# A tuned matmul with batch normalisation on one core: one more small transfer at the head, 64 words of x read through ScalarE's queue

## The chip, the core and the metric

The kernel runs on one core of a Trainium2 chip. The metric is device time in microseconds (us) of one execution, as a median of several executions of the same kernel. The kernel before was measured three times: 205.70, 205.74 and 206.15 us, median 205.74 us. The profile is of one execution, recorded on the chip.

## What is computed

```python
y = np.matmul(x, weight)                             # x: 16 x 512 x 1024, weight: 1024 x 768, float32
mean = np.mean(y, axis=(0, 1), keepdims=True)
var = np.var(y, axis=(0, 1), keepdims=True)
return gamma * (y - mean) / np.sqrt(var + eps) + beta
```

x is 8192 rows of 1024 words (33.5 MB), the weights are 3.1 MB, the result is 8192 x 768 words (25.2 MB). The statistics of each of the 768 columns run over all 8192 rows, so no row of the result can be written before the whole product is known.

## The kernel before

**Tiles.** The 8192 rows are worked on as 16 chunks of 512 rows (`CH`, `C`). The 768 columns are six tiles of 128. For the first two column tiles the product is made with rows on the partitions (`mm_rows`, line L510: x is the loaded operand, the weights are the moving one); for the other four with columns on the partitions (`mm`, L575: the weights are loaded, x is moving). The inner dimension of 1024 is cut into four quarters of 256 (`KQ`), each on 32 partitions, and each quarter into four steps (`jw`) of two halves (`e`): eight matmuls of 128 deep add up to one result.

**Loads.** GpSimd (POOL) issues all loads of x and of the weights, and each of them turns float32 into bf16 on its way. `load_x` (L403) makes four transfers of a group of rows, one for each quarter of the inner dimension, and puts them into `ring`; `load_quarter` (L387) moves one quarter of the weights for two of the four `jw` into `w_sb`. The order at the head, written out in the list `order`, with two weight quarters put in by `BETWEEN`, is: weights quarter 0 and 1 (first half of `jw`), x rows 0 to 255 in four transfers, weights quarter 2 and 3, x rows 256 to 511, the second half of the weights, x rows 512 to 767, rows 768 to 1023, and then whole chunks of 512 rows. A transfer of 256 rows reads 1 KB of each row and writes 512 bytes; its packets are counted as "128 KB". A weight transfer is counted as "192 KB", in packets of 3072 bytes. POOL's transfers share eight completion semaphores in turn, so that the ninth waits until the first has landed, and so on.

**Turning x.** VectorE (DVE) turns 32x32 blocks of the loaded x, so that the inner dimension stands on the partitions (`turn_x`, L435 and L428). The first 512 rows are turned in halves of `jw`.

**The order of work.** A planner in the kernel (`arrange`) takes tasks with costs and due times and writes one instruction order for each engine. `seq` fixes that order. The few instructions ahead of the planner's tasks (memsets, the activation below, the four small reads of the weights) stand in the program by hand, and the planner doesn't know of them.

**The head by hand.** ScalarE (ACT) has one small activation (`warm`, L346) whose table load comes with it; nothing reads `warm`. SyncE (SP) then issues four small reads of the weights into a tile `touched` (L350): for each quarter the first word of the rows in the first half of `jw`, 64 words in each transfer. Nothing reads `touched`. TensorE (PE) runs 16 row pieces of matmuls on a tile of zeros (`wake`, L591 and L594: 8 calls in float32, which show as 16, and 8 small ones in bf16) while the first data comes; two more such pieces stand between its first and second part of real work (`FILL`). Then comes `part(0, 1, ...)`: the first 256 rows with the first half of `jw`, first with L510, then with L575.

**Statistics and output.** ACT, DVE and POOL take squares, sums and bn_stats out of PSUM while PE goes on; ACT copies y to bf16 in SBUF. When a column tile's statistics are whole, its y is scaled and shifted, turned back (on PE against an identity, or by DMA transposes that SP issues), and SP stores it. The identity is made by POOL (`make_identity`) between its first loads, and ACT copies it to float32 (`ident32`, L457).

Of the kernel before, what the change touches and what calls it, by code (L numbers as in the profile page):

```python
# [227 lines left out]
def kernel(  # L228
# [9 lines left out]
    nc = tc.nc  # L238
    f32 = mybir.dt.float32
# [8 lines left out]
    P = 128  # L248
# [33 lines left out]
    x_flat = x.flatten_outer_dims()  # L282
    out_flat = out.flatten_outer_dims()

    singles = ctx.enter_context(tc.tile_pool(name="singles", bufs=1))
# [7 lines left out]
    def seq(bi):  # L293

        ins = bi.ins
        prev = last.get(ins.engine)
        if prev is not None:
            tc.add_manual_dep(
                ins, prev,
                mybir.DependencyInfo(mybir.DependencyClass.NoSync, mybir.DependencyReason.DATA),  # L300
                reason="order",
            )
        last[ins.engine] = ins.name
        return bi
# [38 lines left out]
    base = singles.tile([P, 2], f32)  # L343
    fss = singles.tile([P, 2], f32)

    seq(nc.scalar.activation(warm, eps_sb, AF.Sqrt))  # L346
    touched = singles.tile([P, 2, TOUCH], f32)
    first_rows = weight.rearrange("(i jw c e) n -> i c jw (e n)", i=4, jw=JW, e=2)
# [990 lines left out]
    for c, r0, rows in ends:  # L1339
        due = E + 2.0 + 0.6 * c  # L1340
        n = max(rows // CH, 1)
# [70 lines left out]
```

## Time and profile before

| | |
|---|---|
| device time, median of 3 | 205.74 us (205.70 to 206.15) |
| span of the profiled execution, first to last instruction | 204.07 us |
| time around the span (median less span; the profiled execution has no time of its own on record) | 1.67 us |
| PE busy | 189.3 us, 93% of the span |
| DVE, ACT, POOL busy | 78%, 72%, 61% |
| loads: POOL's queue | 18.36 MB as written, in 34624 packets |
| mean granted TensorE clock | 0.979 |

All times inside the profile count from the first instruction of the span. A slice of the page's rows is a fortieth of the span, 5.1 us. "DMA" in such rows is the busy share of the 16 DMA engines, and GB/s counts the bytes that were written: for loads of x and of the weights half the bytes that were read, since they become bf16. L-numbers are lines of the kernel before; in the changed kernel the lines behind the insertion are higher by three.

### The profile page before, as it was taken

The page shows a single profiled execution, that of the slowest core. Times are in us where ns is not written, and L with a number is a line of the kernel's source. Part 1 is how long each engine was busy: PE and PEld are TensorE (multiplying, and loading weights), DVE is VectorE, ACT ScalarE, POOL GpSimd, SP SyncE. Part 2 cuts the span into 40 slices and gives each one's busy share as a digit, 9 for nine tenths or more (in the row PEclk, how much of TensorE's full clock was granted, in tenths as well). Part 3 has the DMA queues.
Part 4 walks back from the last instruction along what each step waited for, and adds up shares of the span by engine and source line. Part 5 has one row for each costly group of instructions (what it writes and reads, how often), then busy time and mean ns, then how long its engine had stood idle before and what let it go on. Part 6 is the DMA issues. An engine that isn't in the chain of part 4 may idle for free.

```text
span 204.1 us, 3510 instructions
## 1 busy us (share of the span) xinstructions
PE 189.3 (93%) x1210; PEld 114.5 (56%) x1210; DVE 159.3 (78%) x250; ACT 146.2 (72%) x260; POOL 124.1 (61%) x150
## 2 busy tenths in 40 slices
PE   7969999999999999999999999999999999997900
PEld 3457554657488888777865444444444445544600
DVE  4031879999999999969989998987999878657900
ACT  2001461368989999899978766999998959956950
POOL 7776954877499989997403999389613312940000
PEclk9999999999999999999999999999999999999965
DMA  4999999999999999999686899899999999999998
GB/s 71 172 199 196 176 196 196 196 197 197 190 193 197 197 196 196 196 197 195 103 181 200 297 339 336 248 301 328 295 322 227 336 303 274 347 343 310 310 347 253
DMA packets 98562, 48.74 MB, mean 239 GB/s; under 512 B 24304, under 2 KB 98032, under 8 KB 98544
## 3 DMA queue, kind: packets, MB, share of 16 engines
q0 software_dynamic: 34624, 18.36, 65.5%
q1 hardware_dynamic: 63920, 30.16, 52.6%
q8 instruction: 9, 0.15, 0.3%
q14 instruction: 9, 0.07, 0.1%
HBM read 36.71 MB, written 25.17 MB: 303 GB/s over the span
## 4 chain that ended last, share of the span: by engine, by line
PE 86%; ACT 3%; DMA 3%; POOL 2%; issue 1%; ACTq 0%; DVE 0%; POOLq 0%
PE y_ps L575 54%; PE y_ps L510 24%; PE y_ps L814 4%; ACT o_sb L1361 3%; DMA ring<-in_x_dram 3%; PE o_ps L1044 1%; POOL ring L403 1%; POOL w_sb L387 1%; PE y_ps L753 1%; PE a_ps L903 1%; PE o_ps L1074 0%; ACTq L1407 0%; PE idle_ps L591 0%; PE tot_ps L871 0%; ACT ring L1252 0%
## 5 line engine op out<-in xcount | busy, mean ns | idle before, releaser
L575 PEld LDWEIGHTS <-w_sb 128*128 128x128 bf16 x520 | 50.3, 97 | 57.6
L575 PE MATMUL y_ps<-xT_sb,w_sb 128*128 128x512 bf16 (+1 forms) x272 | 59.3, 371 | 0.0
L575 PE MATMUL y_ps<-x_pl,w_sb 128*128 128x512 bf16 x248 | 57.4, 379 | 0.0
L403 POOL DMA_DIRECT2D ring<-in_x_dram x76 | 47.2, 626 | 14.4 <-DMA ring<-in_x_dram 5.5
L510 PE MATMUL y_ps<-w_sb,xT_sb 128*128 128x256 bf16 x448 | 50.6, 273 | 1.7 <-DMA ring<-in_x_dram 1.6
L510 PEld LDWEIGHTS <-xT_sb 128*128 128x128 bf16 x448 | 43.5, 98 | 9.4 <-DVE xT_sb L435 2.9
L435 DVE STREAM_TRANSPOSE xT_sb<-ring 128x1024 f32<-128x1024 f32 (+1 forms) x29 | 31.2, 1111 | 14.1 <-DMA ring<-in_x_dram 13.9
L711 DVE BATCH_NORM_STATS2 stats<-y_ps 128x6 f32<-128x512 f32 x46 | 30.9, 687 | 7.7 <-PE y_ps L575 7.2
L715 ACT CAST y_sb<-y_ps 128x512 bf16<-128x512 f32 x51 | 29.0, 593 | 10.4 <-DVE stats L711 6.3
L547 ACT COPY x_pl<-xT_sb 128x1024 bf16<-128x1024 bf16 x32 | 32.8, 1063 | 1.7 <-DVE xT_sb L435 1.7
L942 POOL TENSOR_TENSOR ring<-ring,sum 128x1024 f32<-128x1024 f32 (+1 forms) x11 | 23.8, 2188 | 14.9 <-ACT y_ps L724 10.9
L659 ACT ACTIVATE sq_sb<-y_ps 128x512 f32<-128x512 f32 x28 | 16.3, 610 | 16.2 <-PE y_ps L510 15.9
L666 POOL TENSOR_TENSOR sum<-sum,sq_sb 128x512 f32<-128x512 f32 x20 | 25.6, 1278 | 3.0 <-ACT sq_sb L659 1.7
L662 DVE TENSOR_TENSOR sum<-y_ps,sum 128x512 f32<-128x512 f32 x28 | 18.9, 675 | 6.3 <-ACT sq_sb L659 5.3
L672 ACT CAST y_sb<-y_ps 128x512 bf16<-128x512 f32 x28 | 16.3, 594 | 8.2 <-DVE sum L662 8.0
L1178 POOL TENSOR_TENSOR ring<-ring,sum 128x1024 f32<-128x1024 f32 x6 | 14.8, 2477 | 9.8 <-issue 8.5
L937 DVE TENSOR_TENSOR ring<-y_sb,a_ps 128x1024 f32<-128x1024 bf16 (+1 forms) x16 | 16.7, 1079 | 0.1
L1044 PE MATMUL o_ps<-ident,y_sb 128*128 128x128 bf16 x104 | 13.1, 221 | 1.6 <-DVE y_sb L1348 1.5
L1232 ACT CAST ring<-ring 128x1024 f32<-128x1024 bf16 x13 | 13.8, 1063 | 0.6 <-DMA ring<-y_sb 0.6
L1145 POOL COPY sum<-sum 32x256 f32<-32x256 f32 (+1 forms) x17 | 5.8, 340 | 13.4 <-DVE sum L1142 6.5
L428 DVE STREAM_TRANSPOSE xT_sb<-ring 128x2048 bf16<-128x2048 bf16 x6 | 13.5, 2290 | 0.1
L591 PE MATMUL idle_ps<-idle_sb 128*128 128x512 f32 x18 | 9.6, 688 | 1.5 <-DVE idle_sb L316 1.5
(104 smaller groups left out, 153.7 us busy)
## 6 DMA issues: line engine op xcount, KB each, us to landing
out_dram<-ring SPq DMA_DIRECT2D x37, 512.0 KB, 3.4
ring<-in_x_dram POOLq DMA_DIRECT2D x52, 256.0 KB, 8.8
out_dram<-o_sb SPq DMA_DIRECT2D x6, 512.0 KB, 4.7
ring<-in_x_dram POOLq DMA_DIRECT2D x16, 128.0 KB, 5.9
w_sb<-in_weight_dram POOLq DMA_DIRECT2D x8, 192.0 KB, 6.2
out_dram<-ring SPq DMA_DIRECT2D x6, 256.0 KB, 3.0
ring<-in_x_dram POOLq DMA_DIRECT2D x4, 192.0 KB, 7.8
out_dram<-o_sb SPq DMA_DIRECT2D x3, 256.0 KB, 2.5
```

Source lines behind the costliest of these rows:

```text
L403: bi = seq(nc.gpsimd.dma_start(x_bf[32 * i:32 * i + 32], src[:, :, KQ * i:KQ * (i + 1)]))
L435: seq(nc.vector.transpose(dst, src[:, :, jw0:jw1]))
L510: seq(nc.tensor.matmul(y_ps[:, s], x_of(c, jw, e, t * P, (t + 1) * P), w_sb[:, jw, e, 0:NA], start=(s == 0 and jw == 0 and e == 0), stop=( ...
L547: seq(nc.scalar.copy(dst, pairs) if eng == "ACT" else ENG[eng].tensor_copy(dst, pairs))
L575: seq(nc.tensor.matmul(y_ps, w_sb[:, jw, e, nt * P:(nt + 1) * P], moving(c, jw, e, q0 * QR, q1 * QR, parted), start=(jw == 0 and e == 0 an ...
L659: seq(nc.scalar.activation(sq_sb[:, 0:n], slot.tile[:, 0:n], AF.Square))
L662: seq(nc.vector.tensor_add(sum1, slot.tile[:, 0:n], sum1))
L666: seq(ENG[eng].tensor_add(acc, acc, state["sq"][:, 0:n]))
L711: seq(nc.vector.bn_stats(dst, slot.tile))
L715: seq(nc.scalar.copy(y(nt, c), slot.tile))
L937: seq(nc.vector.tensor_mul(slot.o, y_row[c].y[:, s0:s1], aff[0][:, None, :].to_broadcast([P, n, NA])))
L942: seq(ENG[eng].tensor_add(slot.o, slot.o, row[:, None, :].to_broadcast([P, n, NA])))
```

## The change

Three lines are put ahead of ScalarE's `warm` activation. They make a tile of 128 words, take the first word of every sixteenth row of x's first 1024 rows (64 words, 64 KB apart in memory), and let ScalarE's queue read them into 64 partitions of the tile. Nothing reads the tile.

```diff
     fss = singles.tile([P, 2], f32)
 
+    woken = singles.tile([P, 1], f32)
+    words = x_flat[0:1024, 0:1].rearrange("(h e s) n -> e h (s n)", h=4, e=16)
+    seq(nc.scalar.dma_start(woken[0:64], words[:, :, 0:1]))
     seq(nc.scalar.activation(warm, eps_sb, AF.Sqrt))
```

In the built program the order of instructions on PE, DVE, POOL and SP is the same as before. ACT has one instruction more, ahead of its table load. The completion semaphores of SP's and ACT's transfers are dealt out in turn from one set of eight, so each of SP's transfers now uses the next one of the set, and waits for the transfer that stands as many places back as before, with the new one counted in.

## Prediction

> **What bounds the kernel now.** I first read the page: busy shares, rate of the transfers, and the chain that ended last.
>
> ```profile
> span 204.1 us, 3510 instructions
> ...
> PE 189.3 (93%) x1210; PEld 114.5 (56%) x1210; DVE 159.3 (78%) x250; ACT 146.2 (72%) x260; POOL 124.1 (61%) x150
> ...
> GB/s 71 172 199 196 176 196 196 196 197 197 190 193 197 197 196 196 196 197 195 103 181 200 297 339 336 248 301 328 295 322 227 336 303 274 347 343 310 310 347 253
> ...
> PE 86%; ACT 3%; DMA 3%; POOL 2%; issue 1%; ACTq 0%; DVE 0%; POOLq 0%
> ```
>
> PE is the chain; transfers hold only 3% of it. In the loading phase they run at 196, except in the first two slices and the fifth. Next, PE's waits in the whole trace, and the chain's pieces at the head (start, length, what):
>
> ```profile
> PE y_ps L510 <- DMA ring<-in_x_dram: 1.6, 1, 1.6
> PE o_ps L1044 <- DVE y_sb L1348: 1.5, 1, 1.5
> PE idle_ps L591 <- DVE idle_sb L316: 1.5, 1, 1.5
> ```
> ```profile
> 5.32 0.53 POOL w_sb L387
> ...
> 5.98 6.13 DMA ring<-in_x_dram
> 12.11 0.03 issue
> 12.14 1.03 PE y_ps L510 x8
> ```
>
> After 12.14 PE never again waits for a load. So what the head takes, the kernel takes, us for us, and a head that ends earlier moves everything behind it. The chain names x as the releaser, but the first weight load and matmul of L510 need all four weight quarters, and the fourth was issued at 5.32. The weight transfers' landing, in the stretch that holds the third and fourth:
>
> ```profile
> L387 POOL DMA_DIRECT2D w_sb<-in_weight_dram x2: 534/536/538, 4.8 to 5.3; - x2
> ...
> DMA to landing us min/median/max: 6.3/6.5/6.7
> ```
>
> The fourth quarter landed at 5.32 + 6.7 = 12.0, just ahead of PE's first weight load at 12.11. x's first rows had landed by 10.14 (the fourth transfer, issued at 4.2, took 5.9) and were turned from 10.26 to 11.56. So the head is a queue of transfers in one order: two weight quarters, four of x, two weight quarters. The fourth quarter lands when the bytes before it are through. How fast were they (window; DVE's busy time; clock; share; GB/s)?
>
> ```profile
> 3.60:5.00 1.40, 0.00 (x0) 1.00 1.14 202
> 5.00:6.00 1.00, 0.00 (x0) 1.00 1.15 152
> 6.00:7.00 1.00, 0.00 (x0) 1.00 0.82 91
> 7.00:8.00 1.00, 0.00 (x0) 1.00 1.37 180
> 8.00:9.00 1.00, 0.00 (x0) 1.00 1.37 206
> ...
> 22.00:23.00 1.00, 1.00 (x2) 1.00 1.05 144
> ```
>
> There is a hole at 5 to 8, and the queue was not empty: eight transfers had been issued by 5.85. The trace's packet records place it: x's first packet is written at 5.19, and in the hole single packets of x take 738 and 693 ns, where they later take 60. In the whole load of x I find only one more such hole, at 22 to 25 (144, 171, 179 GB/s in the three windows of 1 us), where the 4096th packet, the end of row 1023, goes by. There a 16 KB instruction fetch at 22.3 takes a part; other such fetches cost about 10 KB of the stream, this hole some 88.
>
> **The change, part by part.**
>
> *ACT's issue.* One DMA instruction ahead of the table load (0.73 to 2.01). Nearest rows: SP's four issues took 403 to 427 ns each, POOL's up to 682 ns. An issue from ACT is not in this trace; I take 0.42. `warm` then ends near 2.65 instead of 2.23. ACT's next work is `ident32` at 7.00, after 4.77 us of idling for POOL's identity. Cost 0; the cover is gone only if the issue takes over 4.7 us.
>
> *The new packets.* SP's four touches made 320 four-byte packets, 80 each (64 words and 16 completions), so the new one makes 80, five for each DMA engine. They took 8 ns each while nothing else ran (1.75 to 2.54) and 22 ns between weight packets. The first weight packet is written at 2.69. The first touch, issued at 0.74, landed after 1.6, at 2.3; a read that ACT issues at 0.73 can be through by then: cost 0. If it is late: 5 x 22 ns = 0.11 us.
>
> *SP's touches.* If SP and ACT hinder each other in issuing, each touch comes up to 0.42 later. The second's packets (1.96 to 2.54) then fall among the first weights': another 0.11. The third and fourth already do (landing after 3.5 and 4.1 us). Upper bound of both 0.2; I take 0.
>
> [...]
>
> *Semaphores, later work.* The instruction order is the same on PE, DVE, POOL and SP. SP's completion semaphores move on by one; its next transfers, gamma's, land from 53.5 us on, long after all of these. Cost 0.
>
> *What it may remove.* The words lie 64 KB apart over exactly the rows between the two holes. If the first hole is a cost of reading a stretch of x for the first time, the touch pays it at 1.7 to 2.7, while the DMA engines wait for the first weights anyway. Size against 194 GB/s (the rate at 21 to 22 and 16 to 17 is 192 to 202): 5 to 6 lacks 42 KB, 6 to 7 lacks 103, 7 to 8 lacks 14; 159/194 = 0.82 us. In 5 to 6 the last touches, the weights' end and x's start mix, so I count on 6 to 8: 117/194 = **0.60 us**. Bounds: 0 and 0.82.
>
> *What is late next.* The fourth quarter at 11.4 instead of 12.0 still lands after x is turned (11.56 less 0.6 is 10.96). PE's filler ends at 10.56, so up to 1.5 could be gained. PE's second part starts at 15.85 behind its own two filler pieces (14.99), and DVE's next turn (14.85) hangs on the same queue, which moves as a whole. Nothing takes the gain back. The second hole stays, and PE does not wait there.
>
> *Sum.* 0 + 0 + 0 - 0.60 on a span of 204.07: 203.47. With the 1.67 that lie around the span, the median of 205.74 becomes **205.1 us**, if that part is the same; no row can look into it.
>
> **The rivals.**
>
> *A, the forecast: the hole is a first-read cost and goes.* For it: only two holes in 33.5 MB, one at the first row, one behind the last row that is touched; the same queue, packets and engines run at 192 to 197 elsewhere. 204.8 to 205.35. Chance 0.45.
>
> *B, the hole is not x's first read, or the touch doesn't remove it.* Against A: x's first transfer already visits all 256 rows, and 206 of its 256 packets were written by 6.0; the deepest second falls on the next transfer, 1 KB further in the same rows. The second half of the weights is not touched, and its first reading (13 to 17) shows no hole. And the first quarters, touched less than 1 us earlier, still began with packets of 735 to 992 ns instead of 247. POOL changes from issuing to computing at both holes too (identity at 5.84, L666 at 22.14), though its later L666 shows none. Then the change costs 0 to 0.2: 205.5 to 206.05, middle 205.75. Chance 0.38. [...]
>
> *C, slower: the touched words hold up the first weights.* The mechanism is a slow first read that stays in front of the weights in the DMA engines. Each engine would have four words of x, 1 MB apart. If a word takes the 0.6 us by which the first weight packets were long (835 in the middle, less 247) and they come one after the other, they last from 1.75 to 4.15. The weights, which else flow at full rate from about 3.5, lose 0.65 or more; if x's hole goes too, the two cancel, if it stays, the time is 206.4, and 206.6 with the 0.2 from above. It decides from a landing of the new transfer behind about 3.5 us. Against it: SP's first touch, on weights not read before, put out its 80 packets within 0.25 us. Chance 0.17, including what the unseen 1.67 us may add for a queue that was not in use.
>
> **How the numbers follow.** The likeliest is A: 205.1. Its own range is 204.8 to 205.35. The range for 8 in 10 takes in A and B, 204.8 to 206.1, and leaves C out. This kernel's measurement tells about 0.2%, 0.41 us, from no change. A lies beyond that nearly whole (0.03 of it within), a little of B could too: faster 0.43, same 0.40, slower 0.17.
>
> **What would show it.** Right: windows 6 to 7 and 7 to 8 near 194, no x packet over 400 ns there, the fourth quarter landing near 11.4, PE's first L510 near 11.5, all later pieces of the chain earlier by the same amount; the hole at 22 still there, 0.6 earlier. B: the 91 still stands at 6 to 7 and L510 starts at 12.1. C: the new transfer lands behind 3.5 us, and the first weight quarter later than the 5.0 of before. The forecast is wrong, too, if PE starts earlier and a wait for x or a slower span later takes the time back.

## The result and the profile after

The changed kernel takes **209.01 us** (median of 5 runs, 208.63 to 209.70) beside 205.82 (5 runs, 205.70 to 206.15): a ratio of 1.0146, interval 1.0126 to 1.0167, 3.2 us slower. The profiled execution took 209.70 with a span of 207.92, so 1.78 lie around the span; nothing is hidden there. Its page:

```profile
span 207.9 us, 3511 instructions
...
PE 189.4 (91%) x1210; PEld 114.6 (55%) x1210; DVE 159.5 (77%) x250; ACT 145.9 (70%) x260; POOL 124.2 (60%) x150
...
GB/s 76 156 198 196 182 196 196 187 194 196 190 194 196 197 198 194 196 197 193 92 154 198 383 340 266 261 339 312 313 290 214 309 318 328 345 345 285 281 285 184
...
PE 78%; DMA 9%; ACT 3%; POOL 2%; DVE 1%; issue 1%; ACTq 0%; DVEq 0%; POOLq 0%
```

PE, DVE, ACT and POOL have the same work and the same busy times as before, so what is new is waiting. The row of rates shows it in two places: the second slice has 156 instead of 172, and near the end, where before had 310 and 347, three slices have 281 to 285.

PE's waits and the pieces of its chain at the head (start, length, what):

```profile
PE y_ps L513 <- DMA ring<-in_x_dram: 1.9, 1, 1.9
...
PE y_ps L513 <- DVE xT_sb L438: 0.5, 1, 0.5
```
```profile
5.31 7.00 DMA w_sb<-in_weight_dram
```

The fourth weight quarter lands at 12.31 instead of 12.0, and PE's first L513 starts at 12.45, 0.31 later than before. At 26 us PE waits another 0.5 for a turned x. With these PE and ACT end their work 0.86 later. The remaining 3.0 of the 3.85 that the span grew lie behind the last matmul: from its start to the end of the span it is 13.2 us, where before had 10.2. There ACT still copies the last tiles of the result until 197.5 (before 196.7), and behind that only stores run. SP's issues (start, length, number), before and then after:

```profile
189.31 10.56 SPq L1364 DMA_DIRECT2D out_dram<-o_sb  x11
```
```profile
190.16 12.50 SPq L1367 DMA_DIRECT2D out_dram<-o_sb  x11
```

Two windows in which these eleven stores are the only transfers (window; DVE's busy time; clock; DMA share; GB/s), before and then after:

```profile
194.00:198.00 4.00, 0.00 (x0) 0.71 1.15 347
198.00:202.00 4.00, 0.00 (x0) 0.50 1.15 347
```
```profile
194.00:198.00 4.00, 0.50 (x2) 1.00 0.93 282
198.00:202.00 4.00, 0.00 (x0) 0.62 0.97 285
```

The stores start 0.85 later and then take 1.9 longer to issue: SP's queue waits for earlier stores of `o_sb` to land, 3.8 us at the longest where before had 1.5. They are the same stores of the same tile, `o_sb`, with 512-byte rows, at 0.81 of the rate (282/347). No instruction was added or moved there. What did move is an address. In the built program `fss`, with 8 bytes of each partition, starts at 66496, the new tile of one word at 66528, and `touched` behind it at 66560 instead of 66528: the new tile takes 32 bytes. It lies ahead of `touched`, and the pools opened behind the single tiles, with `o_sb`, `xT_sb`, `x_pl`, `y_sb` and `r_sb`, move as a whole: `o_sb`'s rows started at a multiple of 512 (66560) and now start at 66592, 32 bytes beyond one. `ring` and `w_sb` lie ahead of the tile and stay.

### The profile page after: what moved, and what is told of

Its sections match the earlier page's. It is cut to its first block, busy times and chain, and to the rows that moved or that the text cites. A ratio compares the mean times of both kernels' runs of the same rounds, so it can differ in the third digit from the quotient of the medians.

```text
span 207.9 us, 3511 instructions
## 1 busy us (share of the span) xinstructions
PE 189.4 (91%) x1210; PEld 114.6 (55%) x1210; DVE 159.5 (77%) x250; ACT 145.9 (70%) x260; POOL 124.2 (60%) x150
## 4 chain that ended last, share of the span: by engine, by line
PE 78%; DMA 9%; ACT 3%; POOL 2%; DVE 1%; issue 1%; ACTq 0%; DVEq 0%; POOLq 0%
PE y_ps L578 50%; PE y_ps L513 21%; DMA w_sb<-in_weight_dram 6%; PE y_ps L817 3%; DMA ring<-in_x_dram 3%; ACT o_sb L1364 3%; PE o_ps L1047 1%; POOL ring L406 1%; PE y_ps L756 1%; POOL w_sb L390 1%; DVE xT_sb L438 1%; PE a_ps L906 1%; PE o_ps L1077 0%; ACTq L1410 0%; PE tot_ps L874 0%
## 5 line engine op out<-in xcount | busy, mean ns | idle before, releaser
L513 PE MATMUL y_ps<-w_sb,xT_sb 128*128 128x256 bf16 x448 | 50.5, 273 | 2.5 <-DMA ring<-in_x_dram 1.9
L513 PEld LDWEIGHTS <-xT_sb 128*128 128x128 bf16 x448 | 43.6, 98 | 10.1 <-DVE xT_sb L438 3.5
```

The costliest lines, as they stand in the source:

```text
L513: seq(nc.tensor.matmul(y_ps[:, s], x_of(c, jw, e, t * P, (t + 1) * P), w_sb[:, jw, e, 0:NA], start=(s == 0 and jw == 0 and e == 0), stop=( ...
```

## The experiments

All ratios are to the kernel before, measured beside each kernel on the same chip. "Tail rate" is the rate in the two windows above, in GB/s; the rates in KB per us, in the expectations and below, count the same bytes in units of 1024, so that 347 GB/s are 339 KB per us.

| kernel | pools moved by | transfer added | median us | ratio (interval) | tail rate |
|---|---|---|---|---|---|
| after | 32 bytes | ACT's 64 words of x | 209.01 | 1.0146 (1.0126 to 1.0167) | 282 to 285 |
| e1 | 0 | the same | 206.57 | 1.0026 (1.0008 to 1.0044) | 347 |
| e2 | 32 | none | 208.58 | 1.0117 (1.0090 to 1.0144) | 285 to 289 |
| e4 | 64 | none | 208.55 | 1.0118 (1.0085 to 1.0150) | 277 to 285 |
| g5 | 128 | none | 207.94 | 1.0090 (1.0071 to 1.0110) | 286 to 288 |
| e3 | 256 | none | 206.05 | 0.9992 (0.9972 to 1.0013) | 347 |
| i1 | 256 | as after | 206.57 | 1.0026 (1.0008 to 1.0043) | 347 |
| h3 | `o_sb`'s rows alone, 32 | none | 208.64 | 1.0129 (1.0109 to 1.0149) | 277 to 288 |
| i2 | 32, `o_sb`'s rows back | none | 207.21 | 1.0054 (1.0035 to 1.0074) | 347 |
| h4 | 32, `o_sb`'s rows back | as after | 207.63 | 1.0069 (1.0042 to 1.0096) | 347 |

### The transfer or the address

**e1: the transfer alone.** The words are read into a tile that was there already.

```diff
+    woken = fss
+    words = x_flat[0:1024, 0:1].rearrange("(h e s) n -> e h (s n)", h=4, e=16)
+    seq(nc.scalar.dma_start(woken[0:64, 0:1], words[:, :, 0:1]))
```

> The touch of x as in the changed kernel, but into 64 words of the tile fss, which exists already and is written only at the end; so no tile behind it moves in SBUF. Theory S (the new 4-byte tile takes 32 bytes and moves the pools behind it from a multiple of 512 bytes to 32 beyond one, and the last eleven stores, which read o_sb out of such a pool, run slower): tail as before, about 339 KB per us from 191 on, PE's end to the span's end about 10.8 us; time 205.8 plus what the head does, 0.3 to 0.9 later in the changed kernel's one profile, so 205.5 to 206.7. Rival T (the touch itself, its queue or its moved semaphores slow the tail): about 209, tail at 278 KB per us.

**e2, e3, e4, g5: the address alone.** No transfer is added; the tile `touched` is made larger, so that the pools behind it move by 32, 256, 64 and 128 bytes (16, 72, 24 and 40 instead of 2).

```diff
-    touched = singles.tile([P, 2, TOUCH], f32)
+    touched = singles.tile([P, 16, TOUCH], f32)
```

> The kernel before with no new transfer; only the tile touched is made 64 bytes per partition instead of 8, so that the pools behind it lie 32 bytes further, as in the changed kernel. Theory S: head as before (first L510 at 12.1), the last stores at about 278 KB per us, time 208.3 to 208.8. Rival T: 205.8, no change.

> The kernel before with touched at 288 bytes, pools moved by 256 bytes. If the stores need their 512-byte rows to start on a multiple of 256 bytes in SBUF: 205.8. If on a multiple of 512: about 208.5. Rival T: 205.8.

> The kernel before with touched at 96 bytes, pools moved by 64 bytes. If a multiple of 64 bytes is enough for the stores: 205.8. If not: 208 to 208.8, and a rate near 278 KB per us in the tail. Rival T: 205.8.

> The kernel before with touched at 160 bytes, pools moved by 128 bytes. 256 cost nothing, 32 and 64 cost 2.4. If rows must start on a multiple of 256 for the full rate: 208.5 and 275 to 280 KB per us in the tail. If 128 is enough: 206.0.

The transfer alone costs 0.44 us (206.57 beside 206.13). A shift of 32, 64 or 128 bytes without any transfer costs 1.9 to 2.45 us; one of 256 bytes costs nothing that can be told. So most of the price is that of the address, and the step lies between 128 and 256 bytes.

The loss doesn't grow with the shift: the stores ran at nearly the same rate at 32 and at 128 bytes, 280 and 281 KB per us, before 339, counted from the trace's packets from 194 to 202 us. Why a start 32, 64 or 128 bytes on costs this and one 256 bytes on doesn't, no run shows.

**i1: the changed kernel with one size changed.** The tile has 64 words instead of one, so the pools move by 256 bytes.

```diff
-    woken = singles.tile([P, 1], f32)
+    woken = singles.tile([P, 64], f32)
```

> The changed kernel itself with one size changed: the new tile has 64 words a row instead of one, so that the pools behind it move by 256 bytes instead of 32; the transfer is the same. If the address is the large part of the price and the one transfer more the small part: 206.4 to 206.7 (1.002 to 1.004), the last stores at 339 KB per us again. If the two parts hinder each other, or the transfer costs more in the changed kernel's own form than in the earlier run without a tile: 207.2 or more with the last stores still at 339.

The time falls from 209.01 to 206.57, the value of e1. The first expectation holds, and the last stores run as before:

```profile
194.00:198.00 4.00, 0.00 (x0) 0.77 1.15 347
```

### Which buffer carries it

**h3: only `o_sb`'s rows start 32 bytes on**, inside their own slot; no address but theirs changes.

```diff
-            o_sb = xtpool.tile([P, count, P], f32, tag="xT")
-            slot.o = o_sb
-            seq(nc.scalar.copy(o_sb, bank.tile))
+            o_sb = xtpool.tile([P, count * P + 8], f32, tag="xT")
+            slot.o = o_sb[:, 8:].rearrange("p (s n) -> p s n", n=P)
+            seq(nc.scalar.copy(slot.o, bank.tile))
```

> The kernel before with nothing moved but the rows of o_sb, which begin 32 bytes inside their slot (the tile is 32 bytes longer, still within its slot). If the start of o_sb's rows carries the whole cost of the moved pools: 208.4 and about 278 KB per us in the tail. If the other moved tiles (xT_sb, x_pl, y_sb, r_sb) share in it: less, 206.0 to 208.

It costs 2.7 us by itself. The landing of the stores and of the DMA transposes of `y_sb` (number, KB, median us to landing), in h3 and then in after:

```profile
out_dram<-o_sb SPq DMA_DIRECT2D x6, 512.0 KB, 6.3
...
r_sb<-y_sb SPq DMA_TRANSPOSE x6, 2.8
```
```profile
out_dram<-o_sb SPq DMA_DIRECT2D x6, 512.0 KB, 6.3
...
r_sb<-y_sb SPq DMA_TRANSPOSE x6, 3.3
```

Before has 4.7 for these stores and 2.8 for these transposes. h3 has the stores' 6.3 without the transposes' 3.3: the stores' price comes from `o_sb` alone, and the transposes show a second one.

**h4 and i2: the pools stay 32 bytes on, and `o_sb`'s rows go back to a multiple of 512.** h4 is the changed kernel with this, i2 is e2 with this, so without the transfer. The rest of the edit is as in h3.

```diff
+            o_sb = xtpool.tile([P, count * P + 120], f32, tag="xT")
+            slot.o = o_sb[:, 120:].rearrange("p (s n) -> p s n", n=P)
```

> The changed kernel, all its tiles where they are, but o_sb's rows begin 480 bytes inside their slot and so on a multiple of 512 again. If the start of o_sb's rows carries the cost: the tail back at 339 KB per us, 206.4 to 206.8. Otherwise 209.

> No new transfer; all pools 32 bytes on, and only o_sb's rows put back to a multiple of 512 bytes inside their slot. If o_sb alone carries the price of the address: 205.7 to 206.3 (0.999 to 1.002), the last stores at 339 KB per us. If another moved buffer costs something too: 206.6 to 207.8 although the last stores run at 339; that would be the 1 us or more that the changed kernel with o_sb put back (207.63) had left.

In both the last stores run at 347 again, but 1.7 us (h4) and 1.2 us (i2) of the medians stay; for h4 neither expectation had that. Their runs spread widely, h4's from 206.66 to 208.87 and i2's from 206.25 to 208.34. So `o_sb` is not the only buffer with a price: i2, which has no new transfer, lies above before beyond its interval. The stretch in which SP does nothing but five DMA transposes shows the other one; SP's issues, before and then i2:

```profile
100.08 6.86 SPq L1106 DMA_TRANSPOSE r_sb<-y_sb  x5
```
```profile
100.34 7.95 SPq L1106 DMA_TRANSPOSE r_sb<-y_sb  x5
```

The transposes' packets of 256 bytes take 17.9 ns there in before, e1, i1 and h3, and 21.0 to 21.2 in after, e2, h4 and i2 (means of the trace's packet records). Three in four packets still take 18 ns at most there; the others, up to 156 ns long, raise the mean. From 125 to 186 us, beside stores, the packets of the other fourteen transposes take 20.7 ns in before, 21.1 in i1 and 24.3 in i2. That stretch doesn't part the kernels, though: h5 (below), whose pools are not moved, has 23.1 there, and after 22.6. i2 then comes to its end with stores waiting in the queue, from the start of the last stretch:

```profile
186.00:190.00 4.00, 3.21 (x12) 1.00 1.15 347
190.00:194.00 4.00, 3.92 (x13) 0.58 1.15 345
```

Before has 291 and 308 in these two windows: there the stores keep up with ACT. That the queue is full because of the longer transposes is a reading that fits and is not shown: no run moved `y_sb` and `r_sb` alone, and h5, whose transposes take 17.9 ns, has 344 in the first of these windows too. The two prices also don't add up: `o_sb` alone costs 2.7, the rest 1.2, both together 2.45 (e2). The intervals of e2 and h3 overlap; why the rest adds nothing there is open.

### The last 0.4 us: what one transfer more costs

e1 and i1 leave 0.44 to 0.54 us for the transfer. Is it ACT's queue, the place at the head, or x?

**f1** lets ACT read the words only behind `ident32` (7.3 us), **f2** lets SP read them ahead of its own touches, **f3** lets ACT read 64 words of the weights instead, **g1** lets SP read the words of x behind beta's loads (55 us). All use the tile `fss`, and `words` as in e1; `again` is the view of the weights that SP's touches read; f1's line stands in place of the one that copies `ident32` alone.

```diff
f1  + task(t, act(0.25), lambda eng: (seq(nc.scalar.copy(ident32, ident)), seq(nc.scalar.dma_start(woken[0:64, 0:1], words[:, :, 0:1]))), [idt])
f2  + seq(nc.sync.dma_start(woken[0:64, 0:1], words[:, :, 0:1]))
f3  + seq(nc.scalar.dma_start(fss[0:32, 0:2], again[0, :, 0:2, 0:TOUCH]))
g1  + seq(nc.sync.dma_start(fss[0:64, 0:1], words[:, :, 0:1]))
```

> The same 64 words of x by ScalarE's queue into fss, but issued behind the copy ident32 (near 7.3 us), when x's first rows are already on their way: no tile moves, and nothing can be prepared for x. The touch without a moved tile cost about 0.5 us (ratio 1.0026). Theory Q (the cost is that ScalarE's queue is used at all, around the span or by its packets): again 206.4 to 206.7. Theory X (the cost lies in reading x ahead of the first weights): 206.1, no change.

> The same 64 words into fss, issued by SP ahead of its four touches of the weights; ScalarE's queue is not used. Theory Q: 206.1 (or 0.1 to 0.4 more, since the four touches move 0.42 back each). Theory X: 206.4 to 207. In both the hole at 5 to 8 stays, if a touch of these words doesn't prevent it.

> ScalarE's queue reads 64 words of the weights (those of SP's first touch) into fss at the same place, and no word of x. Theory Q: 206.4 to 206.7. Theory X: 206.1.

> The kernel before with the same 64 words read into fss, but by SP behind beta's loads (near 55 us), far from the head; ScalarE's queue is not used, and SP's later transfers move on by one semaphore as in the changed kernel. The kernels with one transfer by ScalarE's queue cost 0.35 to 0.55 us wherever it stands and whatever it reads. Theory Q (a queue that was not in use before costs this): 206.0, no change. Theory L (the cost is the moved semaphores of SP's stores, or any transfer more): 206.4 to 206.6.

Measured: f1 206.39, 1.0017 (1.0006 to 1.0029); f2 206.75, 1.0036 (1.0019 to 1.0054); f3 206.50, 1.0022 (1.0009 to 1.0035); g1 206.51, 1.0023 (1.0009 to 1.0038). Each costs something, with either queue, with x or the weights, and at 55 us as at 1, and the four intervals overlap. So neither the head nor a queue that was not in use explains the price.

**h1: eight such reads from 54.5 us on instead of one.** Each waits for the one before, so that the last is issued at 89.2, ahead of the next transfer at 99.7. What one more transfer changes everywhere, in the built program, is which of the eight completion semaphores each later transfer gets; eight more put them back.

```diff
+        for _ in range(8):
+            seq(nc.sync.dma_start(fss[0:64, 0:1], words[:, :, 0:1]))
```

> The kernel before with eight late reads of the 64 words by SP behind beta's loads instead of one: SP's later transfers stand at the same semaphores as before, since there are eight of them in turn. If the 0.4 us of one transfer more come from the moved semaphores: 206.0, no change. If each transfer more costs: 206.5 or more, up to 3 us.

h1 takes 206.03, 0.9999 (0.9984 to 1.0014). Seven transfers more take the price away, which fits the turn of the semaphores and not the number of transfers. This is one run, its interval overlaps that of g1, and no run turned the semaphores without a transfer. How a turn by one costs 0.4 us was not found: in the built program each wait stands where it stood, on the next semaphore of the set; only gamma's loads, early on, wait otherwise.

### The hole at the head

**f4: x later.** The third weight quarter goes ahead of x (`BETWEEN = {0: [0, 1, 2]}` instead of `{0: [0, 1]}`), so that x's first packet is written at 6.05 instead of 5.19.

> The kernel before, with the third weight quarter moved ahead of x's first four transfers, so that x's first packet comes about 1 us later (near 6.2 instead of 5.2); POOL makes the identity at 5.8 as before. Theory H1 (the hole is tied to the first packets of x): the hole moves with x, the window 5 to 6 is near 195, the low ones are 6 to 9. Theory H2 (tied to the time, to POOL's identity at 5.84 or to the last touches of the weights): the low window stays 6 to 7. Time 205.6 to 206.8 by either.

The hole goes with x; the windows of f4 (as above):

```profile
5.00:6.00 1.00, 0.00 (x0) 1.00 1.13 197
6.00:7.00 1.00, 0.00 (x0) 1.00 1.06 87
7.00:8.00 1.00, 0.00 (x0) 1.00 0.90 89
8.00:9.00 1.00, 0.00 (x0) 1.00 1.30 169
```

POOL's identity starts at 5.84 in before and at 5.83 in f4, so the hole follows x's arrival, and not POOL's turn from issuing to computing, which rival B had named too. f4 takes 206.72, 1.0046 (1.0031 to 1.0061).

**g3: a word of every row** of x's first 256, instead of every sixteenth of 1024. **g4:** one group of x more is loaded short (`SHORT = 3` instead of 2), so that the end of row 1023 comes at another time.

```diff
g3  +    words = x_flat[0:256, 0:1].rearrange("(p h) n -> p (h n)", h=2)
g4  -    SHORT = 2
g4  +    SHORT = 3
```

> ScalarE's queue reads one word of each of x's first 256 rows (256 words, 4 KB apart) at the head, into fss. If the hole at x's first packets is a cost of first reading each 4 KB, it goes: windows 5 to 8 near 195, first L510 near 11.4, time 205.7 to 206.0. If no touch of x prevents it: windows as before (152, 91, 180 or lower), first L510 at 12.0 to 12.6, time 206.4 to 206.9.

> The kernel before with SHORT = 3: rows 1024 to 1535 are loaded in groups of 256 too, and whole chunks begin at row 1536 instead of 1024 (the planner writes a slightly different order). It tells what the second hole at 22 to 25 belongs to. If to the place in memory (row 1024): it stays at x's packet 4096. If to the first transfers of 512 rows: it moves to packet 6144, near 33 us. Time 205.5 to 207.

Neither touch takes the hole away. After, and then g3:

```profile
5.00:6.00 1.00, 0.00 (x0) 1.00 0.67 64
6.00:7.00 1.00, 0.00 (x0) 1.00 0.80 99
7.00:8.00 1.00, 0.00 (x0) 1.00 1.27 163
```
```profile
5.00:6.00 1.00, 0.00 (x0) 1.00 1.04 143
6.00:7.00 1.00, 0.00 (x0) 1.00 0.89 86
7.00:8.00 1.00, 0.00 (x0) 1.00 1.21 155
```

g3 takes 206.32, 1.0011 (0.9999 to 1.0022). g4 takes 207.94, 1.0086 (1.0062 to 1.0110): its rate is 192 to 199 from 22 to 26, and 133 on the mean of 26 to 31, although row 1023 ends at 23. So the second hole is not tied to that row. It moved as the second expectation had it: the deepest window, 29 to 30 with 59, holds x's packet 6144, the last ahead of the first transfers of 512 rows, at 29.3 (the expectation put it near 33); in before packet 4096 is the last ahead of them, at 22.9. What makes the rate fall there is open, and so is why it falls from 26 on, 3 us ahead of that packet.

**h5: SP's own touches of the weights taken out**, with `warm` enlarged so that no pool moves.

```diff
-    for i in range(4):
-        seq(nc.sync.dma_start(touched[32 * i:32 * i + 32, 0:2], first_rows[i, :, 0:2, 0:TOUCH]))
```

> The kernel before without SP's four touches of the weights, and with no touch of x (32 bytes are added to the tile warm, so that the pools stay where they are). If touching gains nothing: 205.6 to 206.1, and perhaps less by the 0.4 that one transfer more costs. If the touches of the weights shorten their first packets: the first weight quarter lands later than 4.5 to 5.0, first L510 behind 12.2, time 206.3 to 207.

h5 takes 207.29, 1.0067 (1.0045 to 1.0090), and its PE starts at 13.16. So the kernel is 1.4 us slower without these touches, but not in the way that was expected: the first weight quarter lands 3.5 us behind its issue, at 4.8, where before had 3.7 and 5.0. It is the fourth that comes late, at 13.0, behind a hole of 66, 65 and 148 in the windows from 5 to 8. Four transfers fewer also turn the semaphores by four places, so what the touches themselves are worth is open.

## Why the prediction was wrong

- **The step that failed: "Semaphores, later work. ... Cost 0", and "Nothing takes the gain back".** That step went through instructions, queues and semaphores, and stopped at their order. The prediction's list, part by part, has the transfer but never the tile that it is read into. The tile's 32 bytes cost 2.45 us (e2), over five times what the transfer costs. No rival had it: B and C were both about the head.
- **The term of 0.60 was mis-sized: the runs show none of it.** The hole is tied to x's first packets (f4), which spoke for A, but words of x read ahead don't pay it (after, e1, g3). B named this, "or the touch doesn't remove it", and its own argument fits: x's first transfer had itself visited the rows, and the deepest second fell on the next. The touches of the weights are no proof for A either: without them the kernel loses 1.4 us, yet their first quarter lands no later (h5).
- **The semaphores were seen and priced at nothing.** One transfer more costs 0.35 to 0.7 us wherever it stands (e1, f1, f2, f3, g1, i1; with g3 0.3, within its interval of none), eight cost nothing (h1). The text looked only for a later wait that becomes longer.
- **ACT's issue and the new packets held.** The issue took 0.66 instead of 0.42, ahead of 4 us of idle time; the 80 packets took 8.3 ns each and were written from 2.16 to 2.60, before the first weight packet at 2.67.
- **C had the sign and not the cause.** The new transfer landed at 2.96, below C's point of 3.5, and the first weight quarter landed no later, at 4.65 instead of 4.99 (3.3 to 3.8 us behind its issue in every profile here). That e1 lies at C's price, 206.6, is chance: g1 has it with the transfer at 55 us.
- **The 0.86 that PE lost** in the profiled execution is mostly the head's scatter: kernels whose head is instruction for instruction that of before (e2, e3, e4, g5, h3) started PE's first work anywhere from 11.41 to 12.33. e3, which costs nothing, starts its last matmul at 194.60, 0.73 later than before, so this is no part of the explanation. PE's filler scatters too: the prediction took its end at 10.56, and in these profiles it lies anywhere from 10.50 to 12.05. In e1 PE's first work starts right behind it, at 12.08, so an earlier fourth quarter would have gained nothing in that execution.
- **The sum as the runs give it:** 2.45 (e2) and 0.44 (e1) make 2.9 of the 3.2, and 1.0117 x 1.0026 = 1.0143 beside the measured 1.0146. Within the 2.45, `o_sb` alone accounts for the whole (2.7 in h3); the other moved buffers show a price only where `o_sb`'s rows are back in place (1.2 in i2), for a reason that stays open. i1 removes the first part from the changed kernel itself and leaves the second.

No version was clearly faster than the kernel before; its `o_sb` already starts at multiples of 512.

## What to carry to other kernels

A change that makes a tile is also a change of every address behind it: list the tiles that move, and look at those that DMAs read or write, before the instructions. Where a small tile has to be added in front of the pools, fill it up so that the pools move by 256 bytes, as in i1 (206.57 us; 209.01 where they move by 32), or put the words into a tile that is there (e1, 206.57). When the profile after shows the same instructions with the same busy times and a lower rate of one transfer, compare addresses first.

## What the runs showed of the hardware

- Stores of 512-byte rows from SBUF ran at 339 KB per us where the rows started at a multiple of 512 bytes (before) or 256 bytes beyond one (e3, i1), and at 274 to 281 where they started 32, 64 or 128 bytes beyond (e2, e4, g5). A single packet hardly grew (27.0 ns before, 27.7 in h3); the DMA engines' busy share fell from 1.15 to 0.96 in h3, so by these numbers most of the loss lies between the packets.
- DMA transposes out of `y_sb` and into `r_sb`, both 32 bytes off, took 21.2 ns for a packet on the mean in after instead of 17.9 in before, 18% more, while three in four took no longer than before; which of the two ends pays it wasn't tried.
- One small transfer more costs about 0.4 us in this kernel, by either queue and at 1 or 55 us (0.44 in e1, 0.49 in g1), and eight more cost nothing (ratio 0.9999 in h1). The turn of the completion semaphores fits this; how it would cost time, no run here showed.
- Where x's first packets arrive, the rate falls for one to three us, whatever of x was read before: each of the twenty profiles here has a window of 1 us at 119 GB/s or less there (91 in before, 79 in e1, 86 in g3), and 31 at worst (e4), with 192 to 197 for most of the load behind it. Its depth changes from kernel to kernel where the head's instructions don't (119 in e2, 68 in h3).
